# Squares of the input and the rotary additions: from VectorE and GpSimd instructions to accumulating transfers

## The chip, the cores and the metric

The kernel runs on one core of a Trainium2 chip. The metric is the device time of one execution in microseconds (us). The engines are TensorE (PE; PEld is its weight load), VectorE (DVE), ScalarE (ACT), GpSimd (POOL) and SyncE (SP, which issues most transfers); each has its own instruction queue, worked off in order.

## What is computed

The reference is one step of a streaming encoder layer over 1024 prompt frames and 64 sample frames, with a model width of 1024. The parts that matter here are the norm of the input and the rotary embedding of the retention queries and keys:

```python
def rms_norm(x, g=None):
    xf = x.astype(jnp.float32)
    y = xf * lax.rsqrt(jnp.mean(xf * xf, axis=-1, keepdims=True) + EPS)
...
def rope(x, pos):
...
    return jnp.concatenate([x1 * cos - x2 * sin, x2 * cos + x1 * sin], axis=-1).astype(x.dtype)
...
    q = rope(rq.reshape(B, S, RET_HEADS, RET_DK), pos)
    k = rope(rk.reshape(B, S, RET_HEADS, RET_DK), pos) * (RET_DK ** -0.5)
```

There are four retention heads of width 256, so a head's x1 and x2 are two blocks of 128 features. Everything is in float32; after the projections the kernel goes on with the retention itself, sliding-window attention, cross attention and a gated feed-forward part.

## The kernel before

All activations lie transposed, with 128 features on the partitions and the 1088 frames (1024 and 64) along the free axis. `HALF` is 544 frames, so a tile of 128x544 in float32 is 272 KB. `KT` is 8, the number of blocks of 128 features.

**Linear layers.** `strassen` makes a 256x1024 by 1024x1088 product in seven products instead of eight (P1, P2, P6, P5, P7, P3, P4 on the operands B11, B21, T2, T1, T3, B22, T4, in this order; a call of it is named a pass here). Each product is 24 matmuls in float32 halves (L208, L209, L211) into one of three pairs of PSUM banks; TensorE's order is fixed in the program. ScalarE copies the first product (L280, tile u); VectorE adds the later ones to it (L277) and makes the four results (L659, into a `stage` tile). The weights come as raw 512 KB tiles (`raw`, two buffers); each of the seven weight operands is split in a high part by a cast on ScalarE (L125) and a low part by a subtraction on VectorE (L126). GpSimd forms the four sums of weights (L186, L187, L189, L192) in place, so a raw tile is free for the next load only when all seven operands have been split.

**Squares.** `token_squares` sums x's squares over the eight blocks for each half of the frames. SP loads a block (`xsq`, four buffers that are used in turn), ScalarE squares it (L526), and VectorE adds it to the half's accumulator `rstd` (L528, 14 additions). `token_roots` (L537) sums `rstd` over the partitions by nine tiny matmuls, which stand in TensorE's order inside the first pass of keys of head 1, after its fourth product; the roots of the norm follow from it. The order of the passes is: keys of head 0, queries of head 0 (with the squares beside them), keys of head 1, and so on; from head 1 on the retention's own steps are put between the products.

**Rotary step.** In `rotated`, when both 128-feature results of a half are there (a and b), VectorE makes the four products with cosine and sine (L690 to L693), two of them into further stage tiles, and then b·sin is subtracted from a and a·sin added to b (L695, L696), on VectorE for heads 0 and 1 and on GpSimd for heads 2 and 3. SP (heads 0 and 1) or GpSimd (heads 2 and 3) then stores both tiles (L698, L699). The stage tiles are a ring of eight: four for each half of a pass. There are 16 such pairs: four heads, keys and queries, two halves.

**What sets the order.** A scheduler places the instructions of each engine in one fixed order when the program is built. A wait in an engine's queue holds everything behind it. A DMA's completion is a semaphore as well; in the rows below DMAHW are transfers that SP or ScalarE issued, DMASW those that GpSimd issued, and the engines' own names their instructions.

Of the kernel before, what the change touches and what calls it, by code (L numbers as in the profile page):

```python
# [11 lines left out]
F32 = mybir.dt.float32  # L12
F32R = mybir.dt.float32r
AF = mybir.ActivationFunctionType
ALU = mybir.AluOpType
# [4 lines left out]
P = 128  # L20
D = 1024
KT = D // P
# [18 lines left out]
HALF = T // 2  # L41
# [69 lines left out]
class Kernel:  # L111
# [9 lines left out]
    def store(self, out, in_):  # L121
        self.nc.sync.dma_start(out, in_)
# [394 lines left out]
    def token_squares(self):  # L517

        nc, tags = self.nc, ("kt", "vb", "ss", "st")
        for t in range(2):  # L520
            hs = slice(t * HALF, (t + 1) * HALF)
            for k in range(KT):
                x = self.ra.tile([P, HALF], F32, tag=tags[k % 4], bufs=1, name="xsq")
                self.load(x, self.io["xT"][k, :, hs])
                acc = self.rstd[:, hs]
                nc.scalar.activation(x if k else acc, x, AF.Square)  # L526
                if k:
                    nc.vector.tensor_tensor(out=acc, in0=acc, in1=x, op=ALU.add)  # L528

    def token_roots(self):  # L530

# [95 lines left out]
    def project_phase(self):  # L627
        nc, tc, io = self.nc, self.tc, self.io
        with ExitStack() as ctx:
# [24 lines left out]
            def taken(ps, sb):  # L654
                o = next_stage()
                if sb is None:
                    nc.scalar.copy(o, ps)
                else:
                    nc.vector.tensor_tensor(out=o, in0=ps, in1=sb, op=ALU.add)  # L659
                return flat(o)  # L660
# [17 lines left out]
            def rotated(w, h, j):  # L678

                done = {}  # L680

                def emit(i, t, ps, sb):
                    done[i, t] = taken(ps, sb)
                    if (1 - i, t) not in done:
                        return
                    a, b = done[0, t], done[1, t]
                    cos, sin = (rope[:, i, half(t)] for i in range(2))
                    sa, sb = turn(), turn()
                    tt = nc.vector.tensor_tensor
                    tt(out=sb, in0=b, in1=sin, op=ALU.mult)  # L690
                    tt(out=sa, in0=a, in1=sin, op=ALU.mult)
                    tt(out=a, in0=a, in1=cos, op=ALU.mult)
                    tt(out=b, in0=b, in1=cos, op=ALU.mult)  # L693
                    add = (nc.vector if h < 2 else nc.gpsimd).tensor_tensor
                    add(out=a, in0=a, in1=sb, op=ALU.subtract)  # L695
                    add(out=b, in0=b, in1=sa, op=ALU.add)  # L696
                    store = self.store if h < 2 else nc.gpsimd.dma_start
                    store(self.d_qkv[j, 2 * h, :, half(t)], a)  # L698
                    store(self.d_qkv[j, 2 * h + 1, :, half(t)], b)  # L699
                self.strassen(w, self.ops, emit)  # L700
# [63 lines left out]
            op = ctx.enter_context(tc.tile_pool(name="op", bufs=1, reuse_waits="tile"))  # L764
# [940 lines left out]
    def turn(self, name, group):  # L1705

        if name == "T4":
            self.slots["B12"] = self.slots["T4"]
            name = "B12"
        if name[0] == "B":  # L1710
            self.load_operand(name, group)
# [263 lines left out]
```

## Time and profile before

| | |
|---|---|
| median of 3 runs | 2199.45 us (2199.18 to 2199.67) |
| profiled execution | 2199.31 us, of which the span from first to last instruction is 2197.5 |
| instructions | 41612 |
| granted clock of TensorE, mean | 0.993 |
| DMA moved | 291.86 MB, mean 133 GB/s |
| first squares / last addition of squares | 70.0 us / 110.9 us |
| rotary additions, first to last start | VectorE 87.0 to 166.5 (L696), GpSimd 219.4 to 371.8 (L696) |

The profile gives, for one execution, every instruction with its start, its duration, and what ended the idle time before it. In a timeline's row stand the start, the duration, the engine, the line, the operation, the tiles out<-in, the shape, and in brackets the idle time before with the instruction that ended it. In a row of grouped instructions stand the count, then either minimum, median and maximum in ns, or the busy total and the mean of one. A row of a stretch gives the busy time of each engine with the instruction count, the mean granted clock, the share of the DMA engines' time and GB/s. A row of waits gives total, times, longest. A row of transfers gives the count, the size of each and the median time from issue to landing.

### The profile page before, as it was taken

What the parts mean: (1) busy time and instruction counts of PE and PEld (TensorE: products, weight loads), DVE (VectorE), ACT (ScalarE), POOL (GpSimd) and SP (SyncE); (2) the same over time, 40 slices, a digit from 0 to 9 for tenths busy, and PEclk for the clock granted to TensorE, in tenths of its full rate; (3) what the DMA queues carried; (4) which work ended last, traced back from release to release, by engine and by line L of the source; (5) the groups of instructions that cost most, each with busy time, mean ns of one, the idle gap of its engine ahead of it and who ended that gap; (6) DMA issues with size and microseconds to landing.
All of it is one profiled execution on the core that took longest, in us unless ns stands there. A gap on an engine that the chain in (4) does not pass through costs nothing.

```text
span 2197.5 us, 41612 instructions
## 1 busy us (share of the span) xinstructions
PE 2155.3 (98%) x16388; PEld 2104.3 (96%) x16388; DVE 1596.9 (73%) x2721; ACT 884.3 (40%) x1902; POOL 649.6 (30%) x484
## 2 busy tenths in 40 slices
PE   9999999999999998999999999999999999999988
PEld 9999999999999997889999999999999999999987
DVE  7798878767688668876545555768877767779776
ACT  6434343437444355653233433343223222335433
POOL 2224535352264112320000000016655555431121
PEclk9999999999999999999999999999999999999999
DMA  4533434343455485427443121413433232466332
GB/s 172 185 110 111 149 111 162 121 138 112 136 187 163 143 272 161 134 77 231 129 150 112 40 73 55 140 57 109 146 114 104 96 119 81 150 231 221 111 116 82
DMA packets 160981, 291.86 MB, mean 133 GB/s; under 512 B 21554, under 2 KB 90098, under 8 KB 160658
## 3 DMA queue, kind: packets, MB, share of 16 engines
q1 hardware_dynamic: 151074, 263.42, 37.1%
q0 software_dynamic: 5104, 17.44, 2.2%
q10 hardware_dynamic: 4608, 8.36, 1.0%
q8 instruction: 129, 2.11, 0.4%
q14 instruction: 66, 0.54, 0.1%
HBM read 197.99 MB, written 91.95 MB: 132 GB/s over the span
## 4 chain that ended last, share of the span: by engine, by line
PE 74%; DVE 12%; DMA 6%; issue 3%; ACT 3%; POOL 2%; SPq 0%; DVEq 0%; ACTq 0%; POOLq 0%
PE pq L208 14%; PE pq L211 13%; PE pq L209 13%; PE pd L152 7%; PE pd L154 7%; PE pd L153 7%; DVE wq L126 3%; PE pss L1168 1%; DVE stage L659 1%; DVE B L126 1%; DMA hl<-d_op 1%; DMA raw<-w_down 1%; ACT wq L125 1%; DVE u L277 1%; DMA qs<-d_qkv 1%
## 5 line engine op out<-in xcount | busy, mean ns | idle before, releaser
L126 DVE TENSOR_TENSOR wq<-raw,wq 128x512 fp32r<-128x512 f32 (+1 forms) x498 | 444.8, 899 | 159.4 <-ACT wq L125 157.5
L125 ACT CAST wq<-raw 128x512 fp32r<-128x512 f32 (+1 forms) x498 | 299.6, 612 | 567.3 <-PE pq L211 210.6
L208 PE MATMUL pq<-T,wq 128*128 128x272 f32 x1800 | 496.8, 294 | 13.9 <-ACT wq L125 9.6
L209 PE MATMUL pq<-T,wq 128*128 128x272 f32 x1800 | 491.2, 289 | 0.0
L208 PE MATMUL pq<-B,wq 128*128 128x272 f32 x1550 | 424.3, 292 | 0.5 <-DVE u L277 0.5
L209 PE MATMUL pq<-B,wq 128*128 128x272 f32 x1550 | 420.0, 288 | 1.1 <-DVE B L126 1.1
L211 PE MATMUL pq<-T,wq 128*128 128x272 f32 x1800 | 374.6, 289 | 0.0
L186 POOL TENSOR_TENSOR raw<-raw 128x512 f32<-128x512 f32 (+1 forms) x53 | 79.1, 1493 | 996.1 <-DVE rs_r L316 477.1
L208 PEld LDWEIGHTS pq<-T,wq 128*128 128x128 f32 x1800 | 341.8, 190 | 17.0 <-ACT wq L125 10.3
L209 PEld LDWEIGHTS pq<-T,wq 128*128 128x128 f32 x1800 | 345.1, 192 | 0.0
L211 PE MATMUL pq<-B,wq 128*128 128x272 f32 x1550 | 320.3, 287 | 0.0
L209 PEld LDWEIGHTS pq<-B,wq 128*128 128x128 f32 x1550 | 294.5, 190 | 1.3 <-DVE B L126 1.3
L208 PEld LDWEIGHTS pq<-B,wq 128*128 128x128 f32 x1550 | 291.6, 188 | 1.6 <-issue 1.4
L211 PEld LDWEIGHTS pq<-T,wq 128*128 128x128 f32 x1800 | 281.7, 190 | 0.2
L211 PEld LDWEIGHTS pq<-B,wq 128*128 128x128 f32 x1550 | 240.2, 188 | 0.0
L277 DVE TENSOR_TENSOR u<-pq,u 128x544 f32<-128x544 f32 x174 | 125.1, 719 | 64.7 <-PE pq L211 64.0
L189 POOL TENSOR_TENSOR raw<-raw 128x512 f32<-128x512 f32 (+1 forms) x53 | 75.3, 1421 | 95.5 <-DVE wq L126 91.3
L659 DVE TENSOR_TENSOR stage<-pq,u 128x544 f32<-128x544 f32 x108 | 77.5, 717 | 32.5 <-PE pq L211 21.5
L1196 POOL TENSOR_TENSOR t<-t,den 128x768 f32<-128x768 f32 (+2 forms) x34 | 49.6, 1460 | 126.7 <-DVE den L1194 40.3
L192 POOL TENSOR_TENSOR raw<-raw 128x512 f32<-128x512 f32 (+1 forms) x53 | 76.9, 1452 | 15.6 <-DVE wq L126 12.2
L187 POOL TENSOR_TENSOR raw<-raw 128x512 f32<-128x512 f32 (+1 forms) x53 | 78.1, 1474 | 3.4
L152 PE MATMUL pd<-xc,wq 128*128 128x256 f32 (+1 forms) x256 | 74.6, 291 | 0.3 <-DVE qf L1453 0.3
(411 smaller groups left out, 4742.3 us busy)
## 6 DMA issues: line engine op xcount, KB each, us to landing
hl<-d_op SPq DMA_DIRECT2D x84, 272.0 KB, 4.2
d_op<-stage SPq DMA_DIRECT2D x44, 272.0 KB, 2.3
d_op<-ht SPq DMA_DIRECT2D x44, 272.0 KB, 4.2
raw<-w_gate SPq DMA_DIRECT2D x22, 512.0 KB, 3.5
raw<-w_up SPq DMA_DIRECT2D x22, 512.0 KB, 4.9
raw<-w_down SPq DMA_DIRECT2D x16, 512.0 KB, 4.2
d_gate<-stage ACTq DMA_DIRECT2D x28, 272.0 KB, 2.5
d_qkv<-stage SPq DMA_DIRECT2D x24, 272.0 KB, 2.9
```

The source lines that it names most:

```text
L125: self.last_cast = self.nc.scalar.copy(hi, src).ins
L126: self.last_low = self.nc.vector.tensor_tensor(out=lo, in0=src, in1=hi.bitcast(F32), op=ALU.subtract).ins
L152: mm(ps, wh, xh, start=start, stop=False)
L153: mm(ps, wh, xl, start=False, stop=False)
L154: self.last_mm = mm(ps, wl, xh, start=False, stop=stop).ins
L186: tt(out=a11, in0=a11, in1=a21, op=sub)
L187: tt(out=a21, in0=a21, in1=a22, op=add)
L208: mm(ps[:, c, :HC], w[:, 0, ks], x[:, 0, cs], start=start, stop=False)
L209: mm(ps[:, c, :HC], w[:, 0, ks], x[:, 1, cs], start=False, stop=False)
L211: self.last_mm = mm(ps[:, c, :HC], w[:, 1, ks], x[:, 0, c * HC:(c + 1) * HC], start=False, stop=stop).ins
L277: add = lambda out, a, b: nc.vector.tensor_tensor(out=out, in0=a, in1=b, op=ALU.add)
L659: nc.vector.tensor_tensor(out=o, in0=ps, in1=sb, op=ALU.add)
```

## The change

The 14 additions of squares become accumulating transfers that GpSimd issues, from the squares' tile onto `rstd`. The loop now takes both halves of a block before the next block. The rotary product b·sin is made negative (a multiplication with two operations on VectorE), and the 32 rotary additions of all heads become accumulating transfers onto a and b. That is 46 accumulating transfers of 272 KB, from SBUF to SBUF. A removed line shifts the later ones: L696 and on is one less in the kernel after, where L693 and L695 are the accumulating transfers onto a and b.

```diff
@@ -517,15 +517,15 @@
     def token_squares(self):
 
         nc, tags = self.nc, ("kt", "vb", "ss", "st")
-        for t in range(2):
-            hs = slice(t * HALF, (t + 1) * HALF)
-            for k in range(KT):
-                x = self.ra.tile([P, HALF], F32, tag=tags[k % 4], bufs=1, name="xsq")
+        for k in range(KT):
+            for t in range(2):
+                hs = slice(t * HALF, (t + 1) * HALF)
+                x = self.ra.tile([P, HALF], F32, tag=tags[(2 * k + t) % 4], bufs=1, name="xsq")
                 self.load(x, self.io["xT"][k, :, hs])
                 acc = self.rstd[:, hs]
                 nc.scalar.activation(x if k else acc, x, AF.Square)
                 if k:
-                    nc.vector.tensor_tensor(out=acc, in0=acc, in1=x, op=ALU.add)
+                    nc.gpsimd.dma_start(acc, x, accum_op=ALU.add)
 
     def token_roots(self):
 
@@ -687,13 +687,12 @@
                     cos, sin = (rope[:, i, half(t)] for i in range(2))
                     sa, sb = turn(), turn()
                     tt = nc.vector.tensor_tensor
-                    tt(out=sb, in0=b, in1=sin, op=ALU.mult)
+                    nc.vector.scalar_tensor_tensor(sb, b, -1.0, sin, ALU.mult, ALU.mult)
                     tt(out=sa, in0=a, in1=sin, op=ALU.mult)
                     tt(out=a, in0=a, in1=cos, op=ALU.mult)
+                    nc.gpsimd.dma_start(a, sb, accum_op=ALU.add)
                     tt(out=b, in0=b, in1=cos, op=ALU.mult)
-                    add = (nc.vector if h < 2 else nc.gpsimd).tensor_tensor
-                    add(out=a, in0=a, in1=sb, op=ALU.subtract)
-                    add(out=b, in0=b, in1=sa, op=ALU.add)
+                    nc.gpsimd.dma_start(b, sa, accum_op=ALU.add)
                     store = self.store if h < 2 else nc.gpsimd.dma_start
                     store(self.d_qkv[j, 2 * h, :, half(t)], a)
                     store(self.d_qkv[j, 2 * h + 1, :, half(t)], b)
```

Three places of the order that it changes. First GpSimd's queue from the second pair of weight sums of the keys of head 0 to those of the queries of head 0 (between 56 and 83 us in the trace); `rstd<-xsq` are the squares, `stage` the rotary tiles. Before:

```order
L189 TENSOR_TENSOR raw<-raw 128x512 [waits DVE_49]
L192 TENSOR_TENSOR raw<-raw 128x512 [waits Pool_49]
L186 TENSOR_TENSOR raw<-raw 128x512 [waits DMAHW4_49,DMAHW5_49,DVE_49,Pool_49]
L187 TENSOR_TENSOR raw<-raw 128x512 [waits Pool_49]
L189 TENSOR_TENSOR raw<-raw 128x512 [waits DVE_49]
L192 TENSOR_TENSOR raw<-raw 128x512 [waits Pool_49]
```

After:

```order
L189 TENSOR_TENSOR raw<-raw 128x512 [waits DVE_49]
L192 TENSOR_TENSOR raw<-raw 128x512 [waits Pool_49]
L528 DMA rstd<-xsq 128x544 [waits Activation_49] x2
L186 TENSOR_TENSOR raw<-raw 128x512 [waits DMAHW4_49,DMAHW5_49,DVE_49,Pool_49]
L187 TENSOR_TENSOR raw<-raw 128x512 [waits Pool_49]
L528 DMA rstd<-xsq 128x544 [waits DMASW0_49,Activation_49]
L528 DMA rstd<-xsq 128x544 [waits DMASW1_49,Activation_49]
L189 TENSOR_TENSOR raw<-raw 128x512 [waits DVE_49]
L695 DMA stage_714<-stage_714 128x544 [waits DVE_49]
L528 DMA rstd<-xsq 128x544 [waits DMASW2_49,Activation_49]
L693 DMA stage_714<-stage_713 128x544 [waits DVE_49]
L192 TENSOR_TENSOR raw<-raw 128x512 [waits Pool_49]
```

The squares' transfers stand between the weight sums, and each waits for the landing of the one before it in its half (DMASW) as well as for its square.

Then ScalarE's queue in the pass of queries of head 0, around the copy L280 of its first product (at 86.14 us in the trace); `xsq` are the squares. Before:

```order
L125 CAST wq<-raw 128x512 [waits DMAHW5_49,PE_49]
L526 ACTIVATE xsq<-xsq 128x544 [waits DMAHW3_49,DVE_49]
L526 ACTIVATE xsq<-xsq 128x544 [waits DMAHW4_49,Activation_49]
L125 CAST wq<-raw 128x512 [waits PE_49,Pool_49]
L280 COPY u_1043<-pq 128x544
L526 ACTIVATE xsq<-xsq 128x544 [waits DMAHW5_49,DVE_49]
```

After:

```order
L125 CAST wq<-raw 128x512 [waits DMAHW5_49,DVE_49,PE_49]
L526 ACTIVATE xsq<-xsq 128x544 [waits DMAHW2_49,DMASW2_49,Activation_49]
L280 COPY u_1043<-pq 128x544 [waits DVE_49,PE_49]
L526 ACTIVATE xsq<-xsq 128x544 [waits DMAHW3_49,DMASW3_49,Activation_49]
L125 CAST wq<-raw 128x512 [waits DVE_49,Pool_49]
L125 CAST wq<-raw 128x512 [waits DVE_49,PE_49]
L526 ACTIVATE xsq<-xsq 128x544 [waits DMAHW5_49,DMASW5_49,Activation_49]
```

The squares that stand there waited for VectorE's additions to free a buffer, and now wait for landed transfers; the copy and weight casts stand behind such squares.

Last, TensorE's queue around the tiny matmuls L537 (at 116.81 us in the trace), between the products on T1 (tile T_176) and T3 (tile T_183) of the first keys of head 1. Before:

```order
L211 MATMUL pq<-T_176,wq 128x272 x2
L537 MATMUL pt<-ones,rstd 128x2 x4
L537 MATMUL pt<-ones,rstd 128x2 [waits DVE_49]
L537 MATMUL pt<-ones,rstd 128x2 x3
L537 MATMUL pt<-ones,rstd 64x2
L208 MATMUL pq<-T_183,wq 128x272 [waits DVE_49]
```

After:

```order
L211 MATMUL pq<-T_176,wq 128x272 x2
L537 MATMUL pt<-ones,rstd 128x2 [waits DMASW2_49]
L537 MATMUL pt<-ones,rstd 128x2 x3
L537 MATMUL pt<-ones,rstd 128x2 [waits DMASW5_49]
L537 MATMUL pt<-ones,rstd 128x2 x3
L537 MATMUL pt<-ones,rstd 64x2
L208 MATMUL pq<-T_183,wq 128x272 [waits DVE_49]
```

Their order is the same; the first of each half now waits for the landing of the last transfer of that half, where before one wait for VectorE stood at the second half.

## The prediction

> **What bounds the kernel now.** I read the page's busy shares first, then the stretches in which the change acts (60 to 260 us), then TensorE's waits there, then each engine's timeline around those waits.
>
> ```profile
> span 2197.5 us, 41612 instructions
> PE 2155.3 (98%) x16388; PEld 2104.3 (96%) x16388; DVE 1596.9 (73%) x2721; ACT 884.3 (40%) x1902; POOL 649.6 (30%) x484
> ```
>
> TensorE is busy 98% of the span, so a change that gives it no less work can win only its waits, and can lose whatever it makes TensorE wait. The stretches (busy time of PE, PEld, DVE, ACT, POOL, then granted clock, DMA share, GB/s):
>
> ```profile
> 60.00:120.00 60.00, 57.08 (x439) 56.64 (x439) 49.96 (x70) 22.72 (x39) 13.06 (x8) 0.97 0.57 185
> 120.00:180.00 60.00, 58.62 (x458) 57.81 (x457) 56.51 (x112) 22.03 (x47) 19.38 (x13) 0.98 0.34 112
> 180.00:260.00 80.00, 78.21 (x618) 76.03 (x617) 64.98 (x112) 29.52 (x69) 39.84 (x36) 1.00 0.37 118
> ...
> 90.00:95.00 5.00, 2.64 (x21) 2.42 (x20) 5.00 (x9) 1.32 (x2) 0.00 (x0) 1.00 0.90 256
> 95.00:100.00 5.00, 5.00 (x30) 5.00 (x30) 3.94 (x6) 1.80 (x3) 1.60 (x1) 0.66 0.86 337
> ```
>
> TensorE idles 60.00 − 57.08 = 2.92, 1.38 and 1.79 us, 6.1 in all. Right after the longest pause its clock is 0.66 for 5 us, which costs (1 − 0.66) × 5 = 1.7 more. So 7.8 us is all that relief could give here. TensorE's timeline says who made the pauses:
>
> ```profile
> 85.41 0.36 PE L208 MATMUL pq<-T,wq 128*128 128x272 f32 x1 [0.56 <-DVE stage L659]
> ...
> 94.08 0.39 PE L208 MATMUL pq<-T,wq 128*128 128x272 f32 x1 [2.36 <-DVE u L277]
> ...
> 101.74 0.29 PE L208 MATMUL pq<-T,wq 128*128 128x272 f32 x1
> ...
> 116.81 2.05 PE L537 MATMUL pt<-ones,rstd 128*128 128x2 f32 x18
> 118.78 0.39 PE L208 MATMUL pq<-T,wq 128*128 128x272 f32 x1
> ```
>
> Both are in the first pass of queries, behind VectorE. In its queue additions that the change removes (L528, L695, L696) stand ahead of L277, for which TensorE waits at 94.08:
>
> ```profile
> 90.17 0.72 DVE L695 TENSOR_TENSOR stage<-stage,stage 128x544 f32<-128x544 f32 x1
> ...
> 91.43 0.72 DVE L695 TENSOR_TENSOR stage<-stage,stage 128x544 f32<-128x544 f32 x1
> 92.07 0.69 DVE L126 TENSOR_TENSOR wq<-raw,wq 128x512 fp32r<-128x512 f32 x1
> 92.67 0.72 DVE L528 TENSOR_TENSOR rstd<-rstd,xsq 128x544 f32<-128x544 f32 x1
> 93.31 0.72 DVE L277 TENSOR_TENSOR u<-pq,u 128x544 f32<-128x544 f32 x1
> ...
> 110.90 0.72 DVE L528 TENSOR_TENSOR rstd<-rstd,xsq 128x544 f32<-128x544 f32 x1
> ```
>
> The last sum of squares is done at 110.90 + 0.72 = 111.6; its reader on TensorE, L537, comes at 116.81. So the sums now have 5.2 us of slack.
>
> **The change part by part.** *VectorE loses* 14 additions of squares and 16 of the rotary step, 30 × 0.72 = 21.6 us of its queue between 71 and 167 us. L690 becomes a multiplication with two operations; the nearest row of that form:
>
> ```profile
> L512 DVE SCALAR_TENSOR_TENSOR xg<-xg,gains 128x544 f32<-128x544 f32 x4 | 2.9, 774 | 0.0
> ```
>
> That is 0.05 more than the 0.72 of one multiplication, 16 × 0.05 = 0.9 us of VectorE, against 21.6. *GpSimd* loses 16 additions and gains 46 transfers:
>
> ```profile
> L696 DVE TENSOR_TENSOR stage<-stage x8: 709/718/724, 87.0 to 166.5; 128x544 f32<-128x544 f32 x8
> L696 POOL TENSOR_TENSOR stage<-stage x8: 1343/1362/1898, 219.4 to 371.8; 128x544 f32<-128x544 f32 x8
> ```
>
> ```profile
> L698 POOL DMA_DIRECT2D d_qkv<-stage x8: 549/558/567, 223.2 to 373.5; - x8
> ...
>   DVE stage L659: 4.5, 1
> ...
> DMA to landing us min/median/max: 2.4/2.6/5.1
> ```
>
> GpSimd's account is 46 × 0.56 − 16 × 1.4, +3 us on an engine that is busy 30%: nothing by itself. What counts is that each square's transfer waits for the landing of the one before it in its half: a chain of seven links where VectorE had seven additions of 0.72.
>
> *The unknown, A:* the time from issue to landing of one accumulating transfer of 272 KB. No row shows one. The near rows:
>
> ```profile
> xsq<-xT SPq DMA_DIRECT2D x16, 272.0 KB, 4.1
> d_qkv<-stage SPq DMA_DIRECT2D x8, 272.0 KB, 5.0
> raw<-w_q SPq DMA_DIRECT2D x4, 512.0 KB, 7.3
> ```
>
> ```profile
> q0 software_dynamic: 5104, 17.44, 2.2%
> ```
>
> The last row makes 2.2% × 2197.5 / 17.44 MB = 2.77 us per MB on all 16 engines, 0.77 us for 272 KB (0.279 MB). Lower end: a plain GpSimd store, 2.6. Quiet, with a second read of 0.77: 3.4. In this busy stretch: 5.0 + 0.8 = 5.8. Upper end: 7.3, as for transfers of twice the size in the same stretch. I take 4.6, the middle of 3.4 and 5.8, since the first links run in a stretch with a DMA share of 0.9 and the last in a quieter one.
> The Trainium skill (Collectives: The Full Stack, section "The bandwidth ceiling") says that a DMA addition is slow because of two source reads, not because of the adding; no run here shows it yet. With its fixed 2.0 us plus bytes at 436 GB/s (DMA: Bandwidth & Descriptors, section "Anatomy of one DMA"), two reads make 3.3, an estimate, by which the steps below give −2.7 at L537.
>
> *The chain, in before's times.* These rows carry it:
>
> ```profile
> 70.71 2.07 ACT L526 ACTIVATE xsq<-xsq 128x544 f32<-128x544 f32 x3
> ...
> 86.14 0.61 ACT L280 COPY u<-pq 128x544 f32<-128x544 f32 x1
> ...
> 95.69 1.14 ACT L125 CAST wq<-raw 128x512 fp32r<-128x512 f32 x2 [0.90 <-DMA raw<-w_k]
> ```
>
> ```profile
> 76.66 1.81 POOL L187 TENSOR_TENSOR raw<-raw 128x512 f32<-128x512 f32 x1
> ...
> 98.40 1.65 POOL L186 TENSOR_TENSOR raw<-raw 128x512 f32<-128x512 f32 x1 [15.62 <-DVE stage L659]
> ```
>
> ```profile
> 90.27 0.33 SPq L119 DMA_DIRECT2D raw<-w_k  x1
> ```
>
> 1. Squares k=1 are ready at 72.2 (the second of three from 70.71 on, 2.07 / 3 = 0.69 each) and are issued. GpSimd then does L186 and L187 (to 78.5) and issues k=2 at max(78.5, 72.2 + A).
> 2. A square's buffer is free only when its transfer has landed: 78.5 + A. The load of k=4 (4.1) and its square (0.69) end at 83.3 + A. On ScalarE, in order, the copy L280 of the pass of queries stands behind it and ends at 83.9 + A. It frees the bank pair for the fourth product, which, without the 0.56, is due at 87.75: in time up to A = 3.85, 0.75 late at 4.6.
> 3. Behind it on ScalarE come the other half's square (0.69) and two weight casts (1.14), then VectorE's subtraction (0.69): at 86.4 + A the raw weights are read and SP can load w_k (before: 90.27). Its cast follows 5.4 later as before (95.69 − 90.27) and ends at 92.4 + A; then five VectorE steps of about 0.65 run, the last of them L659, for which the last product of the queries waits: it starts at 95.7 + A, where before it was 101.74. TensorE gains 6.0 − A here, and reaches L537 (116.81 − 101.74 = 15.07 later) at 110.8 + A.
> 4. k=5 goes out when GpSimd has L186 and L187 of w_k behind it (1.65 and about as much for the second, after that cast's subtraction at 93.1 + A, and 0.2 between instructions): 96.6 + A. Then k=6 at 96.6 + 2A and k=7 at 96.6 + 3A; its second half goes out 1.9 later (three issues of 0.56 and the gaps between them) and lands at 98.5 + 4A. The second part of L537 takes 1.1 more (half of 2.05), and the next product starts at the later of 98.5 + 4A + 1.1 and 112.9 + A, against 118.78 before.
>
> So this stage moves by: A = 2.6, 115.5, −3.3; 3.4, 116.3, −2.5; **4.6, 118.0, −0.8**; 5.8, 122.8, +4.0; 7.3, with k=2 1.0 later by step 1, 129.8, +11. The break-even is A = 4.8. The cap for this stage, if nothing were late, is 0.56 + 2.36 + 1.7 = 4.6.
>
> *The passes of head 1 and the first of attention, 120 to 260.* TensorE's waits there:
>
> ```profile
> PE pss L152 <- DVE kt L930: 2.5, 4, 1.1
> ```
>
> Of the idle 1.38 + 1.79 = 3.2 us, VectorE's lost additions may take all or, if what is late next is a transfer that L659 now waits for, none. I take −1.0: some waits have other work of VectorE ahead of them.
>
> *Heads 2 and 3.* A tile of the ring is ready for its store A after its products instead of 1.4 us, 3.2 later. The ring's eight tiles serve one pass of seven products, of which five take the 15.07 above: 21 us, which cover it. Priced at zero, bounds 0 and +2; faster VectorE multiplications there (L690 beside GpSimd's additions) give nothing, since TensorE hardly waits.
>
> Sum: −0.8 − 1.0 = −1.8. The profiled run took 2199.31 (span 2197.5 and 1.8 around it), 0.14 under the median of 2199.45; against the median, 2197.6. A measurement of this kernel can tell about 0.2% (4.4 us) from no change.
>
> **The rivals.** *The chain of transfers becomes the bound at L537 (slower).* From A = 6.1 the total passes +4.4. For it: the stretch from 90 to 100 moves data at shares of 0.90 and 0.86, and SP's 272 KB stores land after 5.0 there. Against it: k=5 to 7 go out after 100, where fewer loads are open. At 7.3: +11 − 1.0, and with a second drop of the clock after the long wait +1.7: 2211. Chance 0.28. A form of it: VectorE's work holds up GpSimd's making of descriptors, so that a link takes up to 1.9 longer, the most that an addition of L696 on GpSimd took beside VectorE: A = 6.5, +7.0 − 1.0, 2205.5. Against it: the eight issues of L698, from 223 us on with VectorE busy 65 of 80, all took 549 to 567 ns.
> The Trainium skill (SBUF — State Buffer, section "SBUF: two separate sides") has this as a trap for transfers that GpSimd issues; its condition is a two-port copy mode, which no row here shows in the additions' place.
>
> *Late stage tiles in heads 2 and 3 (slower).* If a pass's results land later than the ring allows, L659 waits, and with it a bank pair: about 1 us in each of six passes, +6: 2204. For it: L659 on VectorE already waits once for such a store. Chance 0.05.
>
> *Short transfers (faster).* A at 2.6 to 3: −3.3 at L537, and −1.0 to −3.2 after it: −4.3 to −6.5, 2193 to 2195. For it: GpSimd's own stores land in 2.6. Against it: that is from 223 us on, at half the traffic. Chance 0.17.
>
> *The transfers don't replace the additions:* excluded, as the sums have no other writer.
>
> **How the numbers follow.** Forecast case (A of 3.4 to 6.1, changes of −3.5 to +4.4): 0.50, and its likeliest value is 2197.6; its own range is 2196 to 2203.8. The range for 8 in 10 takes in most of the fast case, down to 2193.5, and the chain up to A = 7.3 with the clock drop, 2211. Faster by over 0.2%: 0.17; within: 0.50; slower: 0.28 + 0.05 = 0.33.
>
> **What would show it.** Right: the accumulating transfers land after 3.4 to 6 us; the wait of 2.36 for L277 is gone or smaller; k=7 lands within a microsecond or so of TensorE's arrival at L537. Wrong, slower: a long wait of TensorE at L537 for the last squares, with A over 6 in the rows, or waits for L659 that end with a transfer in heads 2 and 3. Wrong, faster: no wait at L537, A under 3.4 and TensorE idle under 2 us in all from 60 to 260.

## The result

The change makes the kernel slower: 2225.48 us (2224.07 to 2227.90, four runs) against 2199.56; the ratio is 1.012, with a 95% interval of 1.0105 to 1.0136, so +23 to +30 us. The prediction had 2197.6, with a range up to 2211.

### The profile page after: what moved, and what is told of

It reads as the page before. It is cut to its first block, busy times and chain, and to the rows that moved or that the text cites. A ratio compares the mean times of both kernels' runs of the same rounds, so it can differ in the third digit from the quotient of the medians.

```text
span 2223.6 us, 41670 instructions
## 1 busy us (share of the span) xinstructions
PE 2162.2 (97%) x16388; PEld 2109.1 (95%) x16388; DVE 1565.0 (70%) x2691; ACT 884.3 (40%) x1902; POOL 664.4 (30%) x514
## 4 chain that ended last, share of the span: by engine, by line
PE 74%; DMA 9%; DVE 9%; issue 3%; POOL 3%; ACT 2%; SPq 0%; DVEq 0%; ACTq 0%; POOLq 0%
PE pq L208 14%; PE pq L211 13%; PE pq L209 13%; PE pd L152 7%; PE pd L153 7%; PE pd L154 7%; DVE wq L126 2%; DMA stage<-stage 1%; DMA xsq<-xT 1%; DMA raw<-w_down 1%; DMA d_qkv<-stage 1%; PE pss L1167 1%; DMA rstd<-xsq 1%; DMA hl<-d_op 1%; DVE B L126 1%
## 5 line engine op out<-in xcount | busy, mean ns | idle before, releaser
L659 DVE TENSOR_TENSOR stage<-pq,u 128x544 f32<-128x544 f32 x108 | 77.5, 717 | 58.7 <-PE pq L211 27.5
L152 PE MATMUL pd<-xc,wq 128*128 128x256 f32 (+1 forms) x256 | 74.6, 291 | 0.3 <-DVE qf L1452 0.3
```

Of the source, the lines that this page charges most:

```text
L152: mm(ps, wh, xh, start=start, stop=False)
```

## The profile after

The page of the kernel after, its span and the busy time of the engines:

```profile
span 2223.6 us, 41670 instructions
PE 2162.2 (97%) x16388; PEld 2109.1 (95%) x16388; DVE 1565.0 (70%) x2691; ACT 884.3 (40%) x1902; POOL 664.4 (30%) x514
```

VectorE is 32 us less busy, GpSimd 15 more, and neither shows in the time. The stretches of the kernel after (columns as before):

```profile
60.00:120.00 60.00, 52.88 (x394) 52.22 (x393) 36.75 (x47) 21.66 (x36) 28.92 (x28) 0.94 0.97 249
120.00:180.00 60.00, 50.78 (x382) 50.03 (x381) 39.68 (x81) 17.77 (x36) 20.00 (x17) 0.91 0.55 138
180.00:260.00 80.00, 79.17 (x641) 78.56 (x639) 59.71 (x115) 31.02 (x70) 32.36 (x32) 1.00 0.51 148
260.00:420.00 160.00, 151.97 (x1149) 146.57 (x1148) 110.43 (x213) 58.42 (x133) 60.22 (x59) 0.97 0.50 145
```

The last stretch in the kernel before:

```profile
260.00:420.00 160.00, 159.91 (x1270) 156.85 (x1269) 127.43 (x229) 65.38 (x148) 63.66 (x56) 1.00 0.41 131
```

Two columns of the first row belong together: VectorE falls from 49.96 to 36.75, as meant, and the share of the DMA engines' time rises from 0.57 to 0.97. TensorE then idles 7.1 and 9.2 us in the first two stretches (2.9 and 1.4 before), and 8.0 in the last, where it had idled 0.1. Its timeline around L537:

```profile
94.34 0.60 PE L208 MATMUL pq<-T,wq 128*128 128x272 f32 x1 [2.91 <-DVE u L277]
...
103.12 0.36 PE L208 MATMUL pq<-B,wq 128*128 128x272 f32 x1 [4.15 <-DVE u L277]
...
107.74 0.29 PE L208 MATMUL pq<-T,wq 128*128 128x272 f32 x1
...
124.64 1.05 PE L537 MATMUL pt<-ones,rstd 128*128 128x2 f32 x8 [1.67 <-DMA rstd<-xsq]
131.92 2.17 PE L537 MATMUL pt<-ones,rstd 128*128 128x2 f32 x10 [6.22 <-DMA rstd<-xsq]
134.02 0.59 PE L208 MATMUL pq<-T,wq 128*128 128x272 f32 x1
```

The pause at 94 is still there, a second one stands at 103, and at L537 TensorE waits for the last squares, 7.9 us in all. The product after L537 starts at 134.02, where it was 118.78: **+15.2 us in the first stage**. Of this, 12.0 is idle time of TensorE (15.0 us in four pauses, against 2.9 in two). TensorE's order of matmuls is the same in all kernels here, so any matmul can be set beside its twin. A second mark is the last group of scores of the retention (L152, pss<-qs,ks), behind heads 2 and 3:

```profile
440.52 0.36 PE L152 MATMUL pss<-qs,ks 128*128 128x256 f32 x1 [0.57 <-DVE kt L930]
```

```profile
467.26 0.36 PE L152 MATMUL pss<-qs,ks 128*128 128x256 f32 x1
```

The first row is of before, the second of after: +26.7. So heads 1 to 3 add **+11.5**, and nothing that matters comes later: the whole span is 26.1 longer.

**Where the DMA engines' time went.** The queues between 60 and 135 us (packets, MB, share of 16 engines), before and after:

```profile
q1 hardware_dynamic: 5707, 12.03, 48.9%
```

```profile
q0 software_dynamic: 3168, 6.13, 47.1%
q1 hardware_dynamic: 5543, 11.90, 47.0%
```

22 accumulating transfers (14 of squares, 8 rotary) take 47.1% of 75 us: 1.61 us each of all 16 engines, beside 0.77 for a plain transfer of that size. The engines go from half used to nearly full. What it does to each link is in the rows of the squares' additions (first their issues, then issue to landing), and of the loads of w_k from SP to ScalarE's cast:

```profile
L528 POOL DMA_DIRECT2D rstd<-xsq x14: 856/879/1155, 72.6 to 124.9; - x14
...
DMA to landing us min/median/max: 4.0/5.4/9.6
```

```profile
93.08 1.52 SPq L119 DMA_DIRECT2D raw<-w_k  x2
```

```profile
101.00 1.14 ACT L125 CAST wq<-raw 128x512 fp32r<-128x512 f32 x2 [5.62 <-DMA raw<-w_k]
```

A is 5.4, and the load of w_k takes 7.9 to its cast where it took 5.4 before.

**Heads 2 and 3.** One place, on GpSimd, VectorE and TensorE:

```profile
275.62 0.57 POOL L697 DMA_DIRECT2D d_qkv<-stage  x1 [3.63 <-DMA stage<-stage]
```

```profile
281.12 0.72 DVE L659 TENSOR_TENSOR stage<-pq,u 128x544 f32<-128x544 f32 x1 [7.71 <-DMA d_qkv<-stage]
```

```profile
282.38 0.55 PE L152 MATMUL pss<-qs,ks 128*128 128x256 f32 x1 [4.63 <-DVE kt L929]
```

The store waits for an accumulation to land, the next user of that stage tile waits 7.71 us for the store, VectorE's queue stands behind it, and TensorE waits 4.63 us for a VectorE step that has nothing to do with the rotary embedding. Right after this pause its granted clock (the last column but two) is half:

```profile
282.40:288.50 6.10, 6.10 (x28) 6.10 (x29) 4.63 (x8) 0.87 (x2) 2.89 (x2) 0.50 0.44 134
```

That costs 3.1 us more. Between the two marks the clock is also 0.50 from 134.1 to 138.3, behind the wait at L537, and from 411.4 to 414.8: together 6.9 us, against 1.7 in the kernel before (0.57 from 119 to 123). So of the 11.5, 6.5 is idle time (10.3 against 3.8) and about 5 the clock.

## The experiments

Two theories. *Traffic:* the transfers take the DMA engines' time, and everything that is loaded, stored or accumulated beside them comes late. *Chain and queues:* the dependent links, GpSimd's in-order queue and the fixed part of each landing cost the time, whatever is moved. "First stage" is the start of the product after L537 against 118.78, "heads 1 to 3" the further change up to the second mark. Both come from one profiled execution of each kernel; e11 and e12, which are the kernel before up to the first mark, stand at +0.1 and +0.2 there. Ratios are to the kernel before, with 95% intervals.

**e1_squares_dma.** The new `token_squares` in the kernel before.

```diff
-                    nc.vector.tensor_tensor(out=acc, in0=acc, in1=x, op=ALU.add)
+                    nc.gpsimd.dma_start(acc, x, accum_op=ALU.add)
```

> Only the squares are summed by accumulating transfers; the rotary step is as before. Chain theory (seven dependent links, each about 5.4 us, decide at the tiny matmuls L537): the first stage loses as much as in the full change, +15 us. Traffic theory (an accumulating transfer takes about 1.6 us of all 16 DMA engines, and 85 to 130 us was saturated by squares and rotary transfers together): without the rotary ones there is room, links take under 5 us, +4 to +8 us. Both expect nothing lost after 200 us.

1.0003 (0.9995 to 1.0012): no change that can be told, where the traffic theory had +4 to +8 in all. First stage +4.4, heads 1 to 3 −1.2; most of the remaining 3.2 is regained behind the second mark. The landing time's median is still 5.3, over what the traffic theory said, and yet TensorE has no wait for a transfer at L537: seven links of 5.3 us fit. The chain theory's +15 is out.

**e2_rotary_dma.** The old `token_squares` in the kernel after: only the rotary additions are transfers.

> Only the rotary additions are made by accumulating transfers; the squares are summed on VectorE as before. Chain theory: the first stage loses nothing (0 to -2 us), and what the full change lost after 200 us remains, +10 us. Traffic theory: the first stage still loses some, +2 to +5, and the later stages +10: +12 to +15 us. If both losses simply add up, this run and the one with the squares alone sum to +26.

1.0090 (1.0073 to 1.0106), more than either said. First stage +4.1, heads 1 to 3 +14.5. In the first stage e1 and e2 alone cost 4.4 and 4.1, together 15.2: 6.7 us belong to neither.

**e3_no_adds.**

```diff
-                if k:
-                    nc.vector.tensor_tensor(out=acc, in0=acc, in1=x, op=ALU.add)
...
-                    add(out=a, in0=a, in1=sb, op=ALU.subtract)
-                    add(out=b, in0=b, in1=sa, op=ALU.add)
+                    if h > 1:
+                        nc.gpsimd.tensor_tensor(out=a, in0=a, in1=sb, op=ALU.subtract)
+                        nc.gpsimd.tensor_tensor(out=b, in0=b, in1=sa, op=ALU.add)
```

> Leaves out work: the squares of blocks 1 to 7 are not added and the rotary additions of heads 0 and 1 are not made, by any engine. It shows what relief of VectorE is worth by itself, free of transfers. The prediction's cap: -4.6 us in the first stage (both pauses and the clock drop gone) and 0 to -3.2 after it, so -4.6 to -7.8. A rival: another wait is right behind, as the weights' loads or casts, and the gain is under 2 us.

0.9968 (0.9955 to 0.9981), −4 to −10 us; first stage −4.8, heads 1 to 3 −4.1. What the change was after is real: the additions on VectorE do cost this much, and its timeline of TensorE from 84 to 96 us has no pause.

**e4_squares_gpsimd.** `nc.gpsimd.tensor_tensor` for the squares.

> The squares are added on GpSimd by ordinary instructions (14 of about 1.4 us) instead of VectorE; the rotary step is as before. If VectorE's queue is what costs 4.6 us in the first stage: -2 to -4 us. If GpSimd's additions hold up its weight sums, or block VectorE while both read the same memory: 0 to +3 us.

1.0025 (1.0015 to 1.0035), a miss: first stage +7.3. GpSimd's additions took 1.71 us in the median, and the weight sums stand behind them in its queue, which is the likely reason; no run tests it. Taking VectorE's work away won nothing here.

**e5_squares_more_stores.** e1, and for heads 0 and 1 more plain stores:

```diff
+                    if h < 2:
+                        for i in range(2):
+                            store(self.d_more[h, j, 2 * i, :, half(t)], a)
+                            store(self.d_more[h, j, 2 * i + 1, :, half(t)], b)
```

> The squares by accumulating transfers, the rotary additions on VectorE as before, and as much traffic as the rotary transfers of heads 0 and 1 would make: each result tile is stored two more times by SP to memory that nothing reads (extra work; nothing waits for an accumulation of the rotary step). Traffic theory: the DMA engines are full from 85 to 130 us, TensorE waits several us at L537, and the first stage is near +15 us, as in the full change. Queue theory (GpSimd's in-order queue, in which rotary transfers and squares wait behind each other's landings): no wait at L537, +1 to +5 us.

1.0054 (1.0039 to 1.0069). TensorE at L537:

```profile
126.43 0.95 PE L538 MATMUL pt<-ones,rstd 128*128 128x2 f32 x8
131.92 2.17 PE L538 MATMUL pt<-ones,rstd 128*128 128x2 f32 x10 [4.54 <-DMA rstd<-xsq]
134.02 0.59 PE L208 MATMUL pq<-T,wq 128*128 128x272 f32 x1
```

First stage +15.2, as in the full change, without one rotary accumulation. Traffic of that size on top of the squares is enough. That it is the same number is chance: the pauses stand elsewhere, 4.5 us of them at L537 where the full change has 7.9. The extra stores also take places in SP's queue between the loads; what that alone costs was not run.

**e6_tiny_rotary.**

```diff
-                    nc.gpsimd.dma_start(a, sb, accum_op=ALU.add)
+                    nc.gpsimd.dma_start(a[:, :16], sb[:, :16], accum_op=ALU.add)
...
-                    nc.gpsimd.dma_start(b, sa, accum_op=ALU.add)
+                    nc.gpsimd.dma_start(b[:, :16], sa[:, :16], accum_op=ALU.add)
```

> The full change, but each rotary accumulation moves only 16 of 544 columns (leaves the rest of the rotary additions out): the same instructions, queues and waits, 3% of the bytes. Traffic theory: the first stage is like the squares alone, +1 to +5 us, and the waits for stage tiles in heads 2 and 3 shrink with the landing time, in all +2 to +6. Queue theory: the wait at L537 stays, the first stage +12 to +16, in all over +18.

1.0030 (1.0018 to 1.0043), +4 to +9. First stage +5.7, a little over what the traffic theory said, where the full change has +15.2; heads 1 to 3 +0.8 where it has +11.5. The rotary transfers' bytes carry most of both. A wait of 3.1 us at L537 stays.

**e7_first_heads.** Heads 2 and 3 as in the kernel before, the rest as after.

> The squares and the rotary additions of heads 0 and 1 by accumulating transfers; heads 2 and 3 on GpSimd as before. Both theories of the first stage: its +14 us remains (15.7 at the matmul after L537, 14 to 15 by 250 us). What the full change lost after 250 us (+12) goes, if it comes from heads 2 and 3's own transfers: +13 to +16 in all. If it comes from elsewhere (a shifted order), +20 or more.

1.0073 (1.0055 to 1.0091). First stage +14.3, heads 1 to 3 +0.9: the second loss is heads 2 and 3's own.

**e8_sp_stores.**

```diff
-                    store = self.store if h < 2 else nc.gpsimd.dma_start
+                    store = self.store
```

> The full change, but SP stores the results of heads 2 and 3 as well, so that a store that waits for an accumulation no longer holds the next half's accumulations in GpSimd's queue. If that in-order queue makes stage tiles late (VectorE's L659 waited 7.7 and 3.9 us for them): the loss after 250 us falls from +12 to under +4, in all +15 to +19. If the landing times themselves make them late, or SP's queue now holds loads in the same way: +24 or more.

1.0096 (1.0081 to 1.0111). Heads 1 to 3 cost 7.5 instead of 11.5, so GpSimd's queue has a part, but not under 4 as that theory wanted; the first stage is at +17.9, so its total says little.

**e9_half_squares.** Transfers for the second half's squares only, in before's loop order.

```diff
-                if k:
+                if k and t:
+                    nc.gpsimd.dma_start(acc, x, accum_op=ALU.add)
+                elif k:
                     nc.vector.tensor_tensor(out=acc, in0=acc, in1=x, op=ALU.add)
```

> The squares of the second half of the frames by accumulating transfers (7), those of the first half on VectorE, the rotary step as before. Traffic theory: the DMA engines have room (7 x 1.6 = 11 us more in 60 to 120), VectorE is relieved by 5 us: -2 to -4 us, the best version so far. Chain theory: the seven links are as long a chain as in the full change: no gain, 0 to +5.

1.0031 (1.0018 to 1.0044), against the traffic theory: first stage +6.9 with half the transfers and a landing time of 4.1. Here the chain sets the end of the stage: the second half's squares come after the first's, its seven links start at 85 us, and TensorE waits 3.5 us at L537, half of the 6.9.

**e10_two_accumulators.** The full change with four links for seven: blocks 0, 2, 4, 6 and 1, 3, 5, 7 in two accumulators per half.

```diff
+        odd = [self.ra.tile([P, HALF], F32, tag=s, bufs=1, name="odd") for s in ("qs", "ot")]
...
-                acc = self.rstd[:, hs]
+                acc = odd[t] if k % 2 else self.rstd[:, hs]
...
+                if k == KT - 1:
+                    nc.vector.tensor_tensor(out=self.rstd[:, hs], in0=self.rstd[:, hs], in1=acc, op=ALU.add)
```

> The full change, but odd and even blocks are summed in two accumulators per half, added at the end on VectorE: the chain has four links where it had seven, with nearly the traffic of the full change (12 transfers of squares where it had 14). Chain theory: the wait of 8 us for the squares at L537 goes, and the total falls by 6 to 8 us, to +18 to +20. Traffic theory: the engines are as full, the work in front of L537 as late: falls by 0 to 3 us, +23 to +26.

1.0096 (1.0078 to 1.0115). TensorE at L537:

```profile
126.49 2.17 PE L540 MATMUL pt<-ones,rstd 128*128 128x2 f32 x10 [5.73 <-DVE rstd L531]
128.60 0.59 PE L208 MATMUL pq<-T,wq 128*128 128x272 f32 x1
```

First stage +9.8. The shorter chain is worth 5.4 us, between the two theories: the number of links counts once each link is long.

**e11_last_heads.** Only the rotary additions of heads 2 and 3 are transfers.

> Only the rotary additions of heads 2 and 3 by accumulating transfers; squares and heads 0 and 1 as before. If the two losses of the full change are independent: nothing before 220 us, and +10 to +12 after it, with L659 waiting for stores of stage tiles. If the second loss grows out of the first (later loads, a shifted order): +0 to +4.

1.0044 (1.0027 to 1.0061). First stage +0.1, heads 1 to 3 +12.3, and L659 waits 21.1 us in four waits for stores, the longest 7.0: independent of the first loss.

**e12_gpsimd_head1.** `h < 1` for `h < 2` in the choice of the adding engine.

> No accumulating transfers: the kernel before with the rotary additions of head 1 on GpSimd too, where it is busy 19 of 60 us. If VectorE's queue is what makes TensorE idle 1.4 us between 120 and 180: -0.5 to -1.5 us. If GpSimd's longer additions make stage tiles or weight sums late: 0 to +4.

1.0026 (1.0016 to 1.0035), a miss; heads 1 to 3 +6.7. TensorE's longest new pauses are 3.7 us for VectorE's L659 at 149 and 2.3 for its kt at 179; which of GpSimd's later results holds VectorE there was not followed.

**e13_tiny_squares, e14_tiny_all.** The full change with `acc[:, :16], x[:, :16]` for the squares; then e6's edit as well.

> The full change, but each accumulation of squares moves only 16 of 544 columns (leaves the rest of the sums of squares out); the rotary transfers are whole. If the bytes of squares and rotary transfers together fill the engines and that makes the wait at L537: the first stage falls from +15.7 to what the rotary transfers cost alone, +3 to +6, in all +14 to +18. If the chain of issues and landings makes it, whatever it moves: the first stage stays over +10.

> The full change with 16 of 544 columns in every accumulation, squares and rotary (leaves the rest out): all instructions, waits and queues, 3% of the bytes. Traffic theory: the first stage shows the relief of VectorE, -2 to -6 us, heads 2 and 3 lose 2 to 4 for the landings that remain, in all -3 to +2. If queues, waits and the fixed part of a landing were the cost: +8 or more.

e13: 1.0091 (1.0074 to 1.0108), +20 in the middle of it, where the traffic theory had +14 to +18; but first stage +2.5, no wait for a transfer at L537, and heads 1 to 3 +17.1. That is 4.8 over e11: with TensorE less late, it feels waits for VectorE in head 1 (2.7 us for L659, 2.1 for kt) that the full change had hidden behind its first loss. e14: 0.9999 (0.9990 to 1.0009), first stage −1.6, heads 1 to 3 +0.9. With every instruction, wait and queue of the change in place and 3% of its bytes, the loss of 26 us is gone. It isn't a gain either: of the 4.8 us that e3 shows for the first stage, queues and fixed landing times eat 3.2.

**e15_blocks_first.** Before, with the loop order of the change alone.

> The kernel before with the change's loop order alone (both halves of a block before the next block), additions on VectorE. It tells the order's part in the squares run (+0.7 us in all, +4.8 at the matmul after L537): if the order matters little, within 2 us of the kernel before; if the order made the squares run better or worse than its transfers, 3 us or more to either side.

0.9993 (0.9984 to 1.0001): the order has no part that can be told in the total. First stage +1.1, heads 1 to 3 −1.3.

**The first stage in one view.** The stretch from 85 to 130 us, one row per kernel, in this order: before, e14, e13, e1, e6, e10, e5, after.

```profile
85.00:130.00 45.00, 42.23 (x311) 42.01 (x312) 42.45 (x74) 14.68 (x26) 12.00 (x7) 0.92 0.44 141
```

```profile
85.00:130.00 45.00, 42.72 (x326) 42.31 (x327) 34.25 (x61) 14.71 (x26) 23.18 (x23) 0.96 0.55 151
```

```profile
85.00:130.00 45.00, 40.26 (x304) 39.40 (x303) 29.09 (x43) 15.30 (x26) 22.98 (x23) 0.96 0.81 200
```

```profile
85.00:130.00 45.00, 38.37 (x277) 37.53 (x278) 32.93 (x50) 15.97 (x28) 16.66 (x16) 0.92 0.82 216
```

```profile
85.00:130.00 45.00, 37.31 (x260) 36.76 (x260) 26.21 (x40) 14.71 (x26) 22.72 (x23) 0.89 0.90 217
```

```profile
85.00:130.00 45.00, 35.08 (x242) 34.55 (x241) 25.28 (x38) 14.47 (x25) 23.01 (x22) 0.85 0.99 242
```

```profile
85.00:130.00 45.00, 31.62 (x221) 30.70 (x220) 29.45 (x40) 11.66 (x20) 14.18 (x14) 0.89 1.02 294
```

```profile
85.00:130.00 45.00, 31.91 (x224) 30.98 (x223) 24.14 (x31) 14.65 (x24) 20.95 (x21) 0.90 1.05 249
```

The last column but one is the share of the DMA engines' time: 0.44, 0.55, 0.81, 0.82, 0.90, 0.99, 1.02, 1.05. The first stage moves by 0, −1.6, +2.5, +4.4, +5.7, +9.8, +15.2, +15.2 us. (By these rows the share can pass 1, so it is a measure of load.) The two go together, and steeply near 1; GpSimd's busy time, the fifth of the busy figures, doesn't order them (14.18 in e5, 23.18 in e14). e2 (0.71, +4.1), e7 (1.06, +14.3) and e8 (1.01, +17.9) fit as well. e9 doesn't: its share is 0.70, and half of its +6.9 is the chain's wait. The order alone proves no cause; e6 and e14, which change only the bytes, do that.

## Why the prediction was wrong

**What bounds the kernel, and what relief is worth.** Right: a cap of 4.6 us for the first stage and 7.8 in all; e3 measured −4.8 and a ratio of 0.9968.

**A.** Forecast 4.6, bounds 2.6 to 7.3; measured 5.4 in the median, 4.0 to 9.6. The size was off by 0.8, and by the prediction's own formula A = 5.4 gives about +2.4 (98.5 + 4 × 5.4 + 1.1 = 121.2 against 118.78). The stage lost 15.2. So the median of A isn't where it failed. The prediction's estimate of 3.3, worked out from the figures of the Trainium skill (DMA: Bandwidth & Descriptors, section "Anatomy of one DMA") with two reads, is close to the shortest landing in the kernel after, 3.4 us for a rotary transfer, and far from the median. Two slips in the sums change nothing: A = 3.3 gives −2.6 at L537, not −2.7, and A = 6.1 gives +4.2 in all, not +4.4.

**The step that failed** is the one under "The unknown, A": the second read of 0.77 us was added to the latency of the transfer alone. It is time of the 16 engines that every other transfer shares. Together, 22 × 1.61 = 35 us were put into 75 us that were half full, and then the loads came late. In step 3 "the other half's square" doesn't follow right behind the copy: its load took 6.4 us (84.7 to 91.1), ScalarE waited 3.6 for it, and so the pause at 94 stayed. And "Its cast follows 5.4 later as before" no longer held: 7.9, where e14 with 3% of the bytes has 4.3. The formula of step 3 puts the last product of the queries at 95.7 + 5.4 = 101.1; it started at 107.7, behind the pause at 103.12, in which VectorE waited for that cast. The chain ended not at 98.5 + 4A = 120.1 but at 131.9. e5 shows it by putting the traffic back without the rotary accumulations, e6 and e14 by taking the bytes away and leaving the rest. That the last links run in a quieter stretch, the reason given for taking the middle, was wrong by the same omission: in the row of the kernel after the share is 1.05 up to 130 us.

The Trainium skill (Collectives: The Full Stack, section "The bandwidth ceiling") has the reason, that an addition needs two source reads, and the trace agrees: 1.61 us against 0.77 for the same bytes, 2.1 times. The prediction cited it and drew a latency from it, where the page speaks of throughput.

**A second term that failed** is in step 4: "its second half goes out 1.9 later (three issues of 0.56 and the gaps between them)". The two last links went out 7.4 apart, with two rotary transfers between them:

```profile
117.47 0.88 POOL L528 DMA_DIRECT2D rstd<-xsq  x1 [1.41 <-ACT xsq L526]
118.81 0.87 POOL L693 DMA_DIRECT2D stage<-stage  x1 [0.46 <-DVE wq L126]
120.50 0.86 POOL L695 DMA_DIRECT2D stage<-stage  x1 [0.82 <-issue]
124.91 0.86 POOL L528 DMA_DIRECT2D rstd<-xsq  x1 [3.55 <-issue]
```

The last link's square was ready at 116.6 and the link before it had landed at 118.5, but it went out at 124.91, 0.3 after the first of the three transfers above it had landed (at 124.6). In no run are more than three accumulating transfers in flight, and ten of the kernel's issues up to 125 us come 0.3 after a landing that leaves two. It looks like a limit of three, and no run tests it. From 119.7, when GpSimd had issued the one at 118.81, the last link is 5.2 late: an estimate of the most that this cost of the 15.2. It grows with the landing times too, and so with the bytes. e5 has no more than two in flight, so its loss is not this. How the 15.2 splits between the two terms stays open.

**The chain as the rival.** "The chain of transfers becomes the bound at L537 (slower)" named the place, the wait of 7.9 us there, and the condition, A over 6.1; it came with a median A below that. The chain has a part, 5.4 us of the 15.2 by e10 and 3.5 of the 6.9 in e9.

**Heads 2 and 3.** Priced at zero because the ring of eight tiles "serves one pass ... 21 us, which cover it". Refuted: +11.5, by e11 independent of the first stage. A row that spoke against it was quoted, and read past: before, L659 already waited 4.5 us for such a store, so there was no slack at that place. That wait itself didn't grow (3.9 us in the kernel after); the 7.71 stands at the next pass, where before there was none. The rival "Late stage tiles" had the mechanism and a chance of 0.05; it comes not as 1 us in each of six passes but as few long stalls in VectorE's queue, of which TensorE feels those that hold its operands. Their sum decides nothing: L659's waits for stores of stage tiles come to 26.7 us in the kernel after and 6.7 before, but to 28.2 in e6 and 24.0 in e14, where heads 1 to 3 lose 0.8 and 0.9. The prediction also left out here that a long pause costs clock, about 5 of the 11.5. e8 gives GpSimd's in-order stores 4.0 of the 11.5; e6 shows that the rest goes with the bytes. How much of that rest is landing time and how much is load on the engines was not separated.

**GpSimd's account.** An accumulating issue took 0.88 us, not 0.56, so the forecast of +3 us on GpSimd became +14.8. By e14, where these issues stay, it costs nothing that can be told in the total.

**The descriptor form of the rival** (a link held up by VectorE's work) isn't needed: the tiny transfers of e14 land in 2.0 to 6.3 us beside the same VectorE, though single issues took up to 1.7 us there.

## What to carry to other kernels

A transfer has two prices: how late it is for the one who waits for it, and how much of the shared engines' time it takes from all others. Add up the second for the stretch in which it runs, beside the share of DMA time that the profile already shows there, before pricing any wait. Count also how many such transfers one queue must have in flight. And where a ring of tiles already shows one wait, don't price a longer hold of a tile at zero: look what stands behind each wait in that engine's queue, and whether TensorE needs it.

No version that does all the work beats the kernel before beyond its interval. e3 says what is left to win, 4 to 10 us; neither GpSimd's instructions nor transfers won any of it here.

## What the runs showed of the hardware

- An accumulating transfer of 272 KB within SBUF takes 1.61 us of all 16 DMA engines (47.1% of 75 us for 22 of them; 1.63 in e1), a plain one 0.77. It lands after 4.0 us at the least in the squares of the kernel after; with 16 columns, 8 KB, after 2.0 at the least and 3.2 in the median (e14's squares).
- GpSimd spends 0.87 to 0.88 us in the median on issuing an accumulating transfer in the kernel after, 0.56 on a plain one in the kernel before (L698). With 16 columns it is no less: medians of 0.87 to 1.15 in e14.
- In none of the runs are more than three accumulating transfers in flight at once; whether that is a limit was not tested.
- After TensorE's pause of 4.63 us its granted clock was 0.50 from 282.4 to 288.5; after the 2.36 us in the kernel before, 0.66 over five us.
- Squares added on GpSimd took 1.71 us in the median (1.36 to 1.84) beside a busy VectorE; the rotary additions of heads 2 and 3 in the kernel before, of the same shape, 1.36 (L696) and 1.49 (L695).
